# A third plain unit per later feed-forward stage, paired first blocks in the down projections, and modulation products moved

## The chip, the cores and the metric

The kernel runs on one core of one Trainium2 chip. The metric is the device time of one execution in microseconds (us). Tables and rows name the engines as the profile does: PE is TensorE (matmuls), PEld its weight loads, DVE is VectorE, ACT is ScalarE, SP is SyncE, which here only starts DMAs.

## The reference

The computation is a two-layer encoder on one sequence of 512 tokens, 1024 channels wide. Each layer has a feed-forward stage, a mixer and a second feed-forward stage, all on a residual stream `x` and all modulated by a conditioning vector `c`:

```python
def adaln_in(x, g, m, i):
    return rmsnorm(x, g) * (1 + m[:, i, 1][:, None]) + m[:, i, 0][:, None]

def swiglu(h, w1, w3, w2):
    return (jax.nn.silu(h @ w1) * (h @ w3)) @ w2

def reference(x, c, ...):
    cond = jax.nn.silu(c)
    for l in range(DEPTH):
        m = (cond @ w_mod[l] + b_mod[l]).reshape(bsz, 3, 3, D_MODEL)
        x = x + 0.5 * m[:, 0, 2][:, None] * swiglu(adaln_in(x, norm_g[l, 0], m, 0), ...)
        h = adaln_in(x, norm_g[l, 1], m, 1) @ w_in[l]
        ...   # mixer: attention beside a short convolution (layer 0) or a long FFT convolution (layer 1)
        x = x + m[:, 1, 2][:, None] * (mix @ w_out[l])
        x = x + 0.5 * m[:, 2, 2][:, None] * swiglu(adaln_in(x, norm_g[l, 2], m, 2), ...)
    return x
```

The hidden width of a feed-forward stage is 2752: 21 blocks of 128 columns (numbers 0 to 20) and a half block of 64 (number 21). All inputs are float32. The modulation `m` is the product of one vector with `w_mod` (75 MB), which the kernel takes in 144 pieces of 512 KB.

## The kernel before

**Arithmetic.** Every float32 operand is split into a high part in a 4-byte reduced format (`fp32r`) and the rest, and a product takes three matmuls: high by high, high by low, low by high (`mm3`, L222). A weight tile arrives by DMA in a `raw` buffer (four of them); ACT casts it to `wh` (L203) and DVE subtracts to get `wl` (L204). There are five buffers each of `wh` and `wl`.

**Stages.** There are six in a row: feed-forward (0,0), the mixer of layer 0, feed-forward (0,2), feed-forward (1,0), the mixer of layer 1, feed-forward (1,2). The last three feed-forward stages are "later" ones below. Each has three groups g0, g1, g2 of hidden blocks (`GROUPS`, L32: 6, 8 and 8 blocks), and each group has an up phase (L619 to L651) and a down projection (`project`, L347).

**Up phase.** A block is computed in one of two ways. A *plain* unit is two sums of 24 matmuls of 512 columns (L636 to L641). A *seven-product* unit (`up_seven`, L480) uses a Strassen-like scheme with seven products of 12 matmuls of 256 columns, 84 in all; its extra sums of weights are made by DVE (L456, L457, L462, L465), and sums over halves of the tokens once per stage by `token_sums` (L397) and `first_sum` (L435: it overwrites half of `h` with the sum T1, so no plain unit can follow it). `late_t1` puts the product that reads T1 last in its unit. A unit ends with the gated product (`glu`, L542, or `finish`, L510), which gives a pair of tiles in buffers `ga`, `gb`, `gc`; the last unit of a group makes it in two halves of tokens (L518 to L527). In g0 of a later stage, blocks 0 and 1 are plain, then comes the half block 21, then `token_sums` and `first_sum`, then blocks 2, 3 and 4 by seven products.

**Down projection.** For each of eight output blocks `dt`, all hidden blocks of the group (six or eight inputs, three matmuls of 512 columns each; the half block two) are summed in one of two PSUM banks of tag C (L365 to L368), one block in one bank and the next in the other, and DVE adds the result to `x` (`update`, L362), which frees the bank. The last projection of a stage (g2) does blocks 4 to 7 in halves of 256 columns and starts the next norm.

**Modulation products.** `gemv` (L232) starts a 512 KB DMA of `w_mod` into a `raw` buffer and has DVE multiply and sum it (L248). `rate` (L570) says how many are asked for per output block of the projections of g0, g1, g2; `in_up` (L571) in which groups one more is asked for ahead of each up unit.

**Order.** A scheduling framework places the instructions on each engine from priorities and buffer counts; on the chip each engine runs its list in order and waits on semaphores. The order of the code is not the order of the lists, so both are shown where it matters.

## Time and profile before

| | |
|---|---|
| median of 3 runs | 1894.36 us (1890.97 to 1896.87) |
| profiled execution | 1898.68 us, of which 1896.9 us span and 1.8 us around it |
| PE busy | 1831.8 us, 97% of the span, 11736 matmuls |
| DVE busy | 1547.3 us, 82% |
| ACT busy | 987.9 us, 52% |
| DMA | 269.23 MB, mean 142 GB/s |

The shares are means over the whole span. Phases are told by windows of the trace: a window gives its length, the busy time and number of instructions of each engine, the granted clock of TensorE as a share of 2.4 GHz (0.50 is 1.2 GHz), and what the DMA engines did. Matmuls overlap in the records, so a matmul's duration is longer than its step to the next one.

### The profile page before, as it was taken

What the parts mean: (1) busy time and instruction counts of PE and PEld (TensorE: products, weight loads), DVE (VectorE), ACT (ScalarE), POOL (GpSimd) and SP (SyncE); (2) the same over time, 40 slices, a digit from 0 to 9 for tenths busy, and PEclk for the clock granted to TensorE, in tenths of its full rate; (3) what the DMA queues carried; (4) which work ended last, traced back from release to release, by engine and by line L of the source; (5) the groups of instructions that cost most, each with busy time, mean ns of one, the idle gap of its engine ahead of it and who ended that gap; (6) DMA issues with size and microseconds to landing.
All of it is one profiled execution on the core that took longest, in us unless ns stands there. A gap on an engine that the chain in (4) does not pass through costs nothing.

```text
span 1896.9 us, 29947 instructions
## 1 busy us (share of the span) xinstructions
PE 1831.8 (97%) x11736; PEld 1642.3 (87%) x11736; DVE 1547.3 (82%) x2634; ACT 987.9 (52%) x1625; POOL 3.6 (0%) x9
## 2 busy tenths in 40 slices
PE   7999999899998999999989999999999998999999
PEld 5789899787788899898888988979887898898997
DVE  7987889787859978888898997987887879696682
ACT  4435345275947445254553554565788365354461
POOL 0000000000000000000000000000000000000000
PEclk9999999999999999999999999999999998999999
DMA  7752745833321634725516364445222322333231
GB/s 260 270 175 90 263 159 167 308 104 99 96 95 45 200 101 135 254 90 200 190 50 226 135 213 138 144 154 182 79 79 94 124 88 72 105 103 123 81 129 58
DMA packets 83655, 269.23 MB, mean 142 GB/s; under 512 B 10024, under 2 KB 13352, under 8 KB 83514
## 3 DMA queue, kind: packets, MB, share of 16 engines
q1 hardware_dynamic: 81898, 263.13, 41.4%
q0 software_dynamic: 1616, 4.20, 0.6%
q8 instruction: 92, 1.51, 0.3%
q14 instruction: 49, 0.40, 0.1%
HBM read 258.88 MB, written 10.50 MB: 142 GB/s over the span
## 4 chain that ended last, share of the span: by engine, by line
PE 79%; DVE 12%; DMA 5%; ACT 2%; issue 1%; SPq 0%; ACTq 0%; DVEq 0%
PE pA L476 26%; PE pC L358 20%; PE pV L476 4%; PE pA L358 4%; DVE wl L204 3%; DMA raw<-w2b 3%; PE pC L225 2%; PE pC L224 2%; PE pC L226 2%; DVE raw L248 2%; PE pA L225 2%; PE pA L226 2%; PE pA L224 2%; DMA raw<-w_mod 1%; ACT wh L203 1%
## 5 line engine op out<-in xcount | busy, mean ns | idle before, releaser
L203 ACT CAST wh<-raw 128x1024 fp32r<-128x1024 f32 (+2 forms) x390 | 371.6, 954 | 484.4 <-PE pA L476 137.1
L204 DVE TENSOR_TENSOR wl<-raw,wh 128x1024 fp32r<-128x1024 f32 (+2 forms) x390 | 429.7, 1104 | 97.1 <-ACT wh L203 92.2
L476 PE MATMUL pA<-e,wh 128*128 128x256 f32 x1680 | 309.2, 282 | 2.6 <-ACT tl L501 2.5
L476 PE MATMUL pA<-h,wh 128*128 128x256 f32 x1680 | 309.1, 282 | 0.4 <-DVE tc L528 0.4
L476 PEld LDWEIGHTS pA<-e,wh 128*128 128x128 f32 x1680 | 257.6, 189 | 7.3 <-ACT tl L501 3.8
L476 PEld LDWEIGHTS pA<-h,wh 128*128 128x128 f32 x1680 | 259.9, 191 | 1.7 <-DVE tc L528 0.6
L476 PE MATMUL pA<-h,wl 128*128 128x256 f32 x840 | 238.2, 284 | 19.2 <-DVE wl L204 19.2
L358 PE MATMUL pC<-gb,wh 128*128 128x512 f32 (+1 forms) x800 | 231.7, 374 | 7.6 <-ACT gb L203 4.5
L476 PE MATMUL pA<-e,wl 128*128 128x256 f32 x840 | 234.9, 280 | 0.0
L358 PE MATMUL pC<-ga,wh 128*128 128x512 f32 (+1 forms) x648 | 186.3, 376 | 9.3 <-DVE x L362 7.4
L248 DVE SCALAR_TENSOR_TENSOR raw<-raw,cond 128x1024 f32<-128x1024 f32 x144 | 174.9, 1220 | 17.3 <-DMA raw<-w_mod 16.6
L358 PEld LDWEIGHTS pC<-gb,wh 128*128 128x128 f32 x800 | 147.1, 193 | 38.1 <-ACT gb L203 5.9
L476 PEld LDWEIGHTS pA<-h,wl 128*128 128x128 f32 x840 | 159.3, 190 | 19.8 <-DVE wl L204 19.8
L476 PEld LDWEIGHTS pA<-e,wl 128*128 128x128 f32 x840 | 158.4, 189 | 0.0
L358 PEld LDWEIGHTS pC<-ga,wh 128*128 128x128 f32 x648 | 118.2, 193 | 34.6 <-issue 11.6
L358 PE MATMUL pC<-gb,wl 128*128 128x512 f32 (+1 forms) x392 | 145.7, 372 | 0.0
L362 DVE SCALAR_TENSOR_TENSOR x<-pC,mod,x 128x512 f32<-128x512 f32 (+1 forms) x108 | 74.1, 686 | 74.5 <-PE pC L358 74.3
L358 PE MATMUL pC<-ga,wl 128*128 128x512 f32 (+1 forms) x300 | 111.7, 372 | 0.0
L476 PE MATMUL pV<-h,wh 128*128 128x256 f32 x560 | 104.3, 285 | 1.3 <-DVE tc L547 1.3
L203 ACT CAST wh<-e 128x1024 fp32r<-128x1024 f32 x70 | 73.1, 1044 | 60.1 <-DVE e L462 33.5
L225 PE MATMUL pA<-h,wh 128*128 128x256 f32 (+1 forms) x333 | 102.9, 316 | 1.2 <-DVE h L345 1.2
L226 PE MATMUL pA<-h,wl 128*128 128x256 f32 (+1 forms) x333 | 102.7, 313 | 0.0
(317 smaller groups left out, 3620.5 us busy)
## 6 DMA issues: line engine op xcount, KB each, us to landing
raw<-w SPq DMA_DIRECT2D x164, 512.0 KB, 3.5
raw<-w_mod SPq DMA_DIRECT2D x144, 512.0 KB, 4.5
raw<-w2b SPq DMA_DIRECT2D x64, 512.0 KB, 4.1
raw<-w_in SPq DMA_DIRECT2D x36, 512.0 KB, 4.3
raw<-w2a SPq DMA_DIRECT2D x32, 384.0 KB, 3.6
raw<-w_out SPq DMA_DIRECT2D x16, 512.0 KB, 3.5
raw<-w_start SPq DMA_DIRECT2D x8, 512.0 KB, 4.8
xs<-x SPq DMA_DIRECT2D x16, 256.0 KB, 2.5
```

Of the source, the lines that this page charges most:

```text
L203: self.nc.scalar.copy(out=hi, in_=src)
L204: self.nc.vector.tensor_sub(out=lo, in0=src, in1=hi.bitcast(F32))
L224: mm(out, lhsT=wh, rhs=rh, start=start, stop=False)
L225: mm(out, lhsT=wh, rhs=rl, start=False, stop=False)
L226: mm(out, lhsT=wl, rhs=rh, start=False, stop=stop)
L248: nc.vector.scalar_tensor_tensor(out=raw, in0=raw, scalar=1.0, in1=self.cond, op0=ALU.mult, op1=ALU.mult, accum_out=m[:, c : c + 1])
L358: nc.tensor.matmul(ps, lhsT=lh, rhs=r, start=q == 0, stop=q == len(todo) - 1)
L362: nc.vector.scalar_tensor_tensor(out=x, in0=ps, scalar=gate[dt], in1=x, op0=ALU.mult, op1=ALU.add)
L476: self.nc.tensor.matmul(out, lhsT=lh, rhs=rr, start=first and n == 0, stop=n == 11, skip_group_check=True)
```

## The change

Three edits are made.

1. In the three later feed-forward stages block 2 becomes a plain unit; `first_sum` follows it, and block 3 is the first seven-product unit, with `late_t1`.
2. All twelve feed-forward down projections are called with `joint=True`: output blocks 0 and 1 take both C banks, every input but the last is multiplied for block 0, then for block 1, and then the last input for each. In g0 the half block is put ahead of block 4, so that block 4 is the last input.
3. The modulation products: (0,0) and (0,2) ask for one instead of two per output block in g2. One per up unit is asked for in g1 and g2 of (0,0) (before: g2 alone), in g1 and g2 of (0,2) (before: none) and in g1 of (1,0) (before: g1 and g2). There are 144 in all, as before.

```diff
-    def project(self, n_in, weight, rhs, gate, key, order=None, bank="C", gemv=0):
+    def project(self, n_in, weight, rhs, gate, key, order=None, bank="C", gemv=0, joint=False):
...
-        def products(ps, w, c0, c1):
-            todo = []
-            for k in order:
-                todo += rhs[k](self.block(w, k), c0, c1)
-            for q, (lh, r) in enumerate(todo):
-                nc.tensor.matmul(ps, lhsT=lh, rhs=r, start=q == 0, stop=q == len(todo) - 1)
+        def products(ps, w, c0, c1, a=0, b=n_in):
+            for k in range(a, b):
+                todo = rhs[order[k]](self.block(w, order[k]), c0, c1)
+                for q, (lh, r) in enumerate(todo):
+                    nc.tensor.matmul(
+                        ps, lhsT=lh, rhs=r, start=k == 0 and q == 0, stop=k == n_in - 1 and q == len(todo) - 1)
...
         nfull = 4 if key else KT
+        pair = []
+        if joint:
+            for dt in range(2):
+                pair.append((weight(dt), self.ps("C")))
+                products(pair[dt][1], pair[dt][0], 0, T, 0, n_in - 1)
         for dt in range(nfull):
-            w = weight(dt)
-            ps = self.ps(bank[dt % len(bank)])
-            products(ps, w, 0, T)
+            if dt < len(pair):
+                w, ps = pair[dt]
+                products(ps, w, 0, T, n_in - 1)
+            else:
+                w = weight(dt)
+                ps = self.ps(bank[dt % len(bank)])
+                products(ps, w, 0, T)
             update(dt, ps, 0, T)
             self.gemv(gemv)
...
-        rate = {(0, 0): (1, 2, 2), (0, 2): (1, 2, 2), (1, 0): (1, 1, 0), (1, 2): (0, 0, 0)}[l, i]
-        in_up = {(0, 0): (2,), (1, 0): (1, 2)}.get((l, i), ())
+        rate = {(0, 0): (1, 2, 1), (0, 2): (1, 2, 1), (1, 0): (1, 1, 0), (1, 2): (0, 0, 0)}[l, i]
+        in_up = {(0, 0): (1, 2), (0, 2): (1, 2), (1, 0): (1,)}.get((l, i), ())
...
                     if not first:
                         self.token_sums()
-                        self.first_sum()
-                elif first and (g == 0 or f < 8):
+                elif f < 8 and first or f == 2:
...
-                    if f == 7:
+                    if f == (7 if first else 2):
                         self.first_sum()
...
-                        late_t1=f == (8 if first else 2), halves=f == fs[-1])
+                        late_t1=f == (8 if first else 3), halves=f == fs[-1])
...
-            self.project(len(rhs), weight, rhs, self.gate[l, i], key if g == 2 else None, gemv=rate[g])
+            self.project(
+                len(rhs), weight, rhs, self.gate[l, i], key if g == 2 else None, gemv=rate[g],
+                order=[0, 1, 2, 3, 5, 4] if g == 0 else None, joint=True)
```

The next pieces are read from the lists of the two kernels; lines are those of each kernel (a line of `token_sums` or of `up_seven` is ten higher in the changed one, the update is L363 there).

**PE, the start of the down projection of (0,2) g1.** `gc` is the last input, `pC_1391` the bank of output block 0; that of block 1 is `pC_1397` before and `pC_1395` in the change. First before, the end of block 0 and the start of block 1:

```order
L358 MATMUL pC_1391_7793<-gb_1351_7499,wh_1389_7788 128x512
L358 MATMUL pC_1391_7793<-gb_1350_7498,wl_1390_7789 128x512
L358 MATMUL pC_1391_7793<-gc_1369_7626,wh_1389_7788 128x512
L358 MATMUL pC_1391_7793<-gc_1370_7627,wh_1389_7788 128x512
L358 MATMUL pC_1391_7793<-gc_1369_7626,wl_1390_7789 128x512
L358 MATMUL pC_1397_7831<-ga_1236_6760,wh_1395_7826 128x512
L358 MATMUL pC_1397_7831<-ga_1237_6761,wh_1395_7826 128x512
L358 MATMUL pC_1397_7831<-ga_1236_6760,wl_1396_7827 128x512
```

And of the change, from the end of block 1's other inputs to the start of block 2:

```order
L358 MATMUL pC_1395_7788<-gb_1348_7457,wh_1393_7783 128x512
L358 MATMUL pC_1395_7788<-gb_1349_7458,wh_1393_7783 128x512
L358 MATMUL pC_1395_7788<-gb_1348_7457,wl_1394_7784 128x512
L358 MATMUL pC_1391_7760<-gc_1368_7588,wh_1389_7755 128x512
L358 MATMUL pC_1391_7760<-gc_1369_7589,wh_1389_7755 128x512
L358 MATMUL pC_1391_7760<-gc_1368_7588,wl_1390_7756 128x512
L358 MATMUL pC_1395_7788<-gc_1368_7588,wh_1393_7783 128x512
L358 MATMUL pC_1395_7788<-gc_1369_7589,wh_1393_7783 128x512
L358 MATMUL pC_1395_7788<-gc_1368_7588,wl_1394_7784 128x512
L358 MATMUL pC_1403_7837<-ga_1228_6701,wh_1401_7832 128x512
L358 MATMUL pC_1403_7837<-ga_1229_6702,wh_1401_7832 128x512
```

The last input stands behind 42 matmuls instead of 21, and the two banks close three matmuls apart, directly ahead of block 2, which needs the first of them again.

**DVE, the same place.** From the last block's gated product to the update of `x` by output block 0 (L362 before). First before:

```order
L204 TENSOR_TENSOR wl_1402_7865<-raw_1400_7863,wh_1401_7864 128x1024
L204 TENSOR_TENSOR gc_1370_7627<-tc_1380_7643,gc_1369_7626 128x256
L523 TENSOR_TENSOR tc_1380_7643<-pA_1387_7701,tl_1378_7641 128x256
L248 SCALAR_TENSOR_TENSOR raw_1404_7895,mod_1_0_0_6555<-raw_1404_7895,cond_75 128x1024
L525 SCALAR_TENSOR_TENSOR tc_1380_7643<-tq_1379_7642,tc_1380_7643 128x256
L248 SCALAR_TENSOR_TENSOR raw_1405_7898,mod_1_0_0_6555<-raw_1405_7898,cond_75 128x1024
L204 TENSOR_TENSOR gc_1370_7627<-tc_1380_7643,gc_1369_7626 128x256
L204 TENSOR_TENSOR wl_1408_7903<-raw_1406_7901,wh_1407_7902 128x1024
L362 SCALAR_TENSOR_TENSOR x_973_5254<-pC_1391_7793,mod_0_2_16_3445,x_973_5254 128x512
```

And of the change (the update is L363):

```order
L535 SCALAR_TENSOR_TENSOR tc_1380_7610<-tq_1379_7609,tc_1380_7610 128x256
L248 SCALAR_TENSOR_TENSOR raw_1404_7863,mod_1_0_16_7816<-raw_1404_7863,cond_75 128x1024
L204 TENSOR_TENSOR gc_1369_7589<-tc_1380_7610,gc_1368_7588 128x256
L248 SCALAR_TENSOR_TENSOR raw_1405_7866,mod_1_0_16_7816<-raw_1405_7866,cond_75 128x1024
L204 TENSOR_TENSOR wl_1408_7871<-raw_1406_7869,wh_1407_7870 128x1024
L248 SCALAR_TENSOR_TENSOR raw_1410_7901,mod_1_0_16_7816<-raw_1410_7901,cond_75 128x1024
L248 SCALAR_TENSOR_TENSOR raw_1411_7904,mod_1_0_16_7816<-raw_1411_7904,cond_75 128x1024
L261 TENSOR_TENSOR mod_1_0_16_7816<-mod_1_0_16_7816,cols_76 128x8
L264 TENSOR_SCALAR mod_1_0_16_7816<-mod_1_0_16_7816 128x8
L363 SCALAR_TENSOR_TENSOR x_973_5254<-pC_1391_7760,mod_0_2_16_3359,x_973_5254 128x512
L363 SCALAR_TENSOR_TENSOR x_974_5255<-pC_1395_7788,mod_0_2_16_3359,x_974_5255 128x512
L204 TENSOR_TENSOR wl_1414_7911<-raw_1412_7909,wh_1413_7910 128x1024
```

Between the last block's last product (L525, L535) and the first update there stand one L248 before and four now, and the two updates now follow each other. One more L248 stands just ahead of the rows shown of the change.

**DVE, (0,2) g0, around the first seven-product unit before and block 2 as a plain unit now.** `e1`, `e2`, `tq` and `h` are the token sums, `wl_1145` is the first weight tile of block 2 in both kernels. First before:

```order
L204 TENSOR_TENSOR h_1034_5677<-e3_1110_6062,h_1033_5676 128x256
L417 SCALAR_TENSOR_TENSOR tq_1135_6119<-tq_1136_6120,th_1134_6117 128x256
L549 TENSOR_TENSOR ga_1104_6023<-tc_1109_6055,ga_1103_6022 64x512
L204 TENSOR_TENSOR e1_1138_6126<-tq_1136_6120,e1_1137_6125 128x512
L552 CAST ga_1104_6023<-ga_1104_6023 64x512
L204 TENSOR_TENSOR e2_1132_6112<-tq_1135_6119,e2_1131_6111 128x256
L204 TENSOR_TENSOR h_1036_5679<-e3_1110_6062,h_1035_5678 128x256
L204 TENSOR_TENSOR h_1038_5681<-e3_1110_6062,h_1037_5680 128x256
L204 TENSOR_TENSOR h_1040_5683<-e3_1110_6062,h_1039_5682 128x256
L456 TENSOR_TENSOR e3_1143_6143<-raw_1142_6142 128x512
L204 TENSOR_TENSOR wl_1145_6149<-raw_1141_6141,wh_1144_6148 128x1024
```

And of the change:

```order
L557 TENSOR_TENSOR tc_1109_6055<-tc_1109_6055,pA_1108_6030 64x512
L424 SCALAR_TENSOR_TENSOR tq_1136_6120<-e3_1110_6062,th_1134_6117 128x256
L204 TENSOR_TENSOR wl_1145_6137<-raw_1143_6135,wh_1144_6136 128x1024
L559 TENSOR_TENSOR ga_1104_6023<-tc_1109_6055,ga_1103_6022 64x512
L427 SCALAR_TENSOR_TENSOR tq_1135_6119<-tq_1136_6120,th_1134_6117 128x256
L562 CAST ga_1104_6023<-ga_1104_6023 64x512
L204 TENSOR_TENSOR e1_1138_6126<-tq_1136_6120,e1_1137_6125 128x512
L204 TENSOR_TENSOR e2_1132_6112<-tq_1135_6119,e2_1131_6111 128x256
L204 TENSOR_TENSOR wl_1148_6167<-raw_1146_6165,wh_1147_6166 128x1024
```

The first weight tile of block 2 moves ahead of nine instructions of token sums and half-block work, and the weight sum L456 ahead of it is gone; the four splits of T1 into `h` go behind block 2 altogether.

## Rows read from the trace of the kernel before

**Rows 1.** The page: busy time of each engine.

```profile
PE 1831.8 (97%) x11736; PEld 1642.3 (87%) x11736; DVE 1547.3 (82%) x2634; ACT 987.9 (52%) x1625; POOL 3.6 (0%) x9
```

**Rows 2.** Windows, up phase of g0: start:end, length, busy (count), clock, DMA share, GB/s.

```profile
605.58:645.54 39.96, 33.02 (x256) 32.58 (x255) 38.41 (x66) 21.67 (x35) 0.00 (x0) 0.87 0.36 120
966.25:1005.29 39.04, 32.11 (x257) 31.64 (x255) 38.05 (x66) 21.51 (x35) 0.00 (x0) 0.91 0.36 121
1574.54:1614.69 40.15, 33.49 (x256) 32.84 (x255) 36.00 (x61) 21.93 (x36) 0.00 (x0) 0.87 0.31 96
```

**Rows 3.** Windows: eight seven-product units of (1,2) g1; three plain units of (0,0) g1.

```profile
1645.78:1725.77 79.99, 79.99 (x676) 79.74 (x675) 67.09 (x103) 46.74 (x72) 0.00 (x0) 1.00 0.35 113
121.92:155.21 33.29, 33.29 (x145) 27.05 (x144) 21.74 (x32) 10.98 (x17) 0.00 (x0) 1.00 0.31 98
```

**Rows 4.** Timeline, (0,2) g0: start, us, engine, line, operation, tiles [idle before <-releaser].

```profile
605.81 0.39 PE L476 MATMUL pV<-h,wh 128*128 128x256 f32 x2
607.17 0.41 DVE L414 SCALAR_TENSOR_TENSOR tq<-e,th 128x256 f32<-128x256 f32 x1
...
611.85 1.22 DVE L204 TENSOR_TENSOR wl<-raw,wh 128x1024 fp32r<-128x1024 f32 x1
...
613.13 0.58 PE L476 MATMUL pA<-h,wl 128*128 128x256 f32 x1 [6.93 <-DVE wl L204]
```

**Rows 5.** Windows: granted clock after two idle stretches of PE.

```profile
608.20:618.40 10.20, 5.27 (x24) 5.27 (x25) 10.14 (x18) 4.97 (x8) 0.00 (x0) 0.50 0.00 0
1010.90:1014.30 3.40, 3.18 (x8) 2.51 (x9) 2.39 (x5) 0.17 (x1) 0.00 (x0) 0.50 0.54 181
```

**Rows 6.** Windows: down projections of g0, stages (0,0), (0,2), (1,0), (1,2).

```profile
84.33:121.92 37.59, 34.57 (x137) 27.29 (x136) 34.28 (x62) 12.60 (x17) 0.00 (x0) 0.91 0.71 232
645.54:680.17 34.63, 32.57 (x135) 26.09 (x134) 26.47 (x43) 8.24 (x11) 0.00 (x0) 0.95 0.58 192
1005.29:1040.18 34.89, 32.46 (x136) 26.00 (x135) 29.47 (x49) 8.24 (x11) 0.00 (x0) 0.95 0.66 219
1614.69:1645.78 31.09, 31.02 (x136) 24.85 (x135) 20.48 (x32) 7.95 (x10) 0.00 (x0) 1.00 0.34 110
```

**Rows 7.** Windows: down projections of g1, stages (0,0) and (0,2).

```profile
205.54:253.21 47.67, 45.71 (x192) 36.54 (x190) 40.14 (x61) 11.00 (x13) 0.00 (x0) 0.96 0.78 265
760.87:804.81 43.94, 43.91 (x192) 35.42 (x190) 36.02 (x56) 9.75 (x11) 0.00 (x0) 1.00 0.76 260
```

**Rows 8.** Windows: projections of g2, (0,0) and (0,2); a mixer's of like shape.

```profile
334.90:380.18 45.28, 38.80 (x209) 33.62 (x208) 31.91 (x54) 12.61 (x19) 1.24 (x1) 0.92 0.87 311
885.37:927.35 41.98, 37.07 (x207) 32.16 (x205) 31.69 (x52) 12.88 (x19) 0.00 (x0) 0.96 0.75 263
531.07:566.67 35.60, 35.59 (x208) 31.09 (x207) 17.20 (x25) 11.40 (x17) 0.00 (x0) 1.00 0.22 74
```

**Rows 9.** Timeline of PE, start of the projection of (1,0) g0.

```profile
1008.06 0.63 PE L358 MATMUL pC<-ga,wh 128*128 128x512 f32 x2
1011.12 0.80 PE L358 MATMUL pC<-gb,wh 128*128 128x512 f32 x1 [2.43 <-ACT gb L203]
```

**Rows 10.** Waits of the whole run: us in total, times, longest.

```profile
PE pC L358 <- DVE x L362: 7.4, 3, 4.2
DVE raw L248 <- DMA raw<-w_mod: 16.6, 23, 3.1
```

**Rows 11.** Timeline, projection of (0,0) g2: one modulation product on DVE.

```profile
363.81 1.22 DVE L248 SCALAR_TENSOR_TENSOR raw<-raw,cond 128x1024 f32<-128x1024 f32 x1
```

**Rows 12.** Timeline, projection of (1,2) g2: first block's last matmul and its update.

```profile
1853.94 0.40 PE L358 MATMUL pC<-gc,wl 128*128 128x512 f32 x1
...
1854.38 0.75 DVE L362 SCALAR_TENSOR_TENSOR x<-pC,mod,x 128x512 f32<-128x512 f32 x1 [1.02 <-PE pC L358]
```

**Rows 13.** Windows: up phases of (0,0) g2 and (0,2) g1.

```profile
253.21:334.90 81.69, 80.82 (x675) 79.42 (x674) 75.92 (x121) 45.85 (x71) 0.00 (x0) 1.00 0.47 157
680.17:760.87 80.70, 80.16 (x677) 79.71 (x675) 70.47 (x110) 45.73 (x71) 0.00 (x0) 1.00 0.37 120
```

More of the change, by code (lines that the diff above doesn't have):

```diff
@@ L638, in ffn @@
                             self.mm3(ps[s], self.block(w, kt), self.h[kt], kt == 0, kt == KT - 1)
-                        if g == 0:
+                        if first and g == 0:
                             self.gemv(4)
```

## The prediction

> **What bounds the kernel now.** I read the page's busy times first. PE is busy 1831.8 of 1896.9 us and every other engine less than 83% [rows 1], so what there is to win is idle time of PE, 65 us by that row, and time at a lower clock; some of both lies at the start and in the mixers, which the change leaves alone. Then I cut the feed-forward stages into phases with windows and compared phases that do the same work. A seven-product unit takes 80.0 / 8 = 10.0 us and a plain unit 33.3 / 3 = 11.1 us where nothing disturbs them [rows 3]. Against that:
>
> - The up phase of g0 in a later stage is three seven-product units, 30.0 us, and takes 39.96, 39.04 and 40.15 us [rows 2]: 10.0, 9.0 and 10.2 us lost, 29.2 together. The timeline shows where: PE starts the first unit at 605.81, has only high weights, and waits 6.9 us for the first `wl`, which DVE starts at 611.85 because the token sums stand ahead of it [rows 4]. Then the granted clock is 0.50, that is 1.2 GHz, for 10.2 us, part of it idle [rows 5].
> - The down projection of g0 takes 31.1 us in (1,2), where no modulation products run, and 37.6, 34.6 and 34.9 us in the other three [rows 6]: 6.5, 3.5 and 3.8 us lost. In g1, (0,0) takes 47.7 us against 43.9 in (0,2) [rows 7]: 3.7 us. The mechanism by the timeline: from 1008.06 to 1011.12 PE waits for `gb`, the last gated product, as 21 or fewer matmuls of the first output block are too short to cover it [rows 9], and again 3.4 us follow at 0.50 [rows 5].
> - In g2, (0,0) and (0,2) take 45.3 and 42.0 us against 35.6 for a mixer's projection of like shape and nearly the same count of matmuls [rows 8]: 9.7 and 6.4 us. Here two products per output block stand in DVE's list and PE waits for the update that frees a bank, 7.4 us in three waits, the longest 4.2 [rows 10].
>
> Together the projections lose 33.6 us in six places.
>
> **Part 1, block 2 plain.** Its price is 11.1 - 10.0 = 1.1 us of PE in each of three stages. In the changed list of DVE the first `wl` of block 2 stands right behind the sum that starts at 607.17 [rows 4], so it can start near 607.5 and end near 608.7. PE has two long and two short matmuls before it needs it and falls idle near 606.3: a wait of 2.4 us instead of 6.9. The second weight comes after some 3.4 us more of DVE work, inside the 5.5 us that PE needs for the first half. The four T1 splits move behind block 2 and are needed last in block 3. I count slow clock behind it, as behind the wait of 2.43 us in g0's projection [rows 9]: 3.4 us at half [rows 5], worth 1.7. So a stage loses 1.1 + 2.4 + 1.7 = 5.2 instead of 9.7, and three stages gain 29.2 - 15.6 = 13.6 us. Bounds: no wait and no slow clock give 29.2 - 3.3 = 25.9; the wait as long as before (a `wl` that again sits behind the sums) gives 29.2 - 3 x (1.1 + 9.7) = -3.2. I take 13.6, since the place of the `wl` is read from the list.
>
> **Part 2, two blocks together.** The last gated product is now wanted after 42 matmuls of 0.23 us (43.9 us for 192 [rows 7]), 9.7 us, in g0 after 28, 6.4 us. The longest lateness so far was about 3 us past five or seven inputs, so these waits end. What is late next is output block 2: it needs bank 0 again, which closes only 6 matmuls (1.4 us) before. Its update stands in DVE's list behind more than before: in (0,2) g1 five L248 and two `wl` from the last block's first gated step on, where two L248 and two `wl` stood. At 1.22 us for an L248 [rows 11] or a `wl` [rows 4] and some 0.4 us for a small step I sum DVE's work ahead of the first update to (0,0): 7.3, 10.3, 8.9 us for g0, g1, g2; (0,2): 7.8, 10.4, 8.9; (1,0): 7.8, 12.9, 16.6; (1,2): 3.9 in each. The pair, with its last inputs, covers 11.1 us (g0: 7.8), from the end of the up phase; about 1.1 us go for the start of DVE's list and the update itself. So the bank is late by 0.4 us in g2 of (0,0) and (0,2), 0.4 to 1.1 us in g0 and g1 of (0,2) and g0 of (1,0), 2.9 us in g1 of (1,0), and by what DMAs add: L248 waited 16.6 us in 23 cases for its `raw` [rows 10], mostly in such projections, and in (0,0) the DMA share is the highest (0.71 to 0.87 [rows 6 to 8]). I put 3.5 us on g0 and g1 of (0,0), 1.3 on g0 and 1.5 on g1 of (0,2), 1.3 on g0 of (1,0), 2.8 on g1 of (1,0), 3 on its g2, where the filter's own matmuls fill part of 6.6. Slow clock adds 1.7 at the four largest and 0.6 at each of the other three: 8.6. In (1,2), where nothing is queued, the first block's last matmul starts at 1853.94 and the update at 1854.38 ends 0.75 later [rows 12]: 1.2 us, of which three matmuls and the last one's own 0.23 cover 0.9. That leaves 0.35 to 0.4 there and in g2 of (0,0) and (0,2): five times, 2.0 us. Sum: 16.9 + 8.6 + 2.0 = 27.5 us of new waits. Bounds: 12 x 0.4 = 4.8 us if DVE is never late; eight times the longest wait for an update, 4.2 [rows 10], with 1.7 of slow clock, 47 us, plus 2 is 49.
>
> The Trainium skill (Perfetto Trace Analysis, Optimizing Tensor Performance, Matmuls) says that independent groups of matmuls should rotate through PSUM banks, so that one is emptied while the next group runs; the pair breaks this, as both banks close together. The trace agrees as far as it goes [rows 12]: the emptying that was hidden there is 0.4 us in the open, 4.8 us for twelve projections by that rule alone.
>
> **Part 3, modulation products.** With one product per block in g2 of (0,0) and (0,2), DVE has 1.3 us less per output block, and the bank waits there go, as in the g1 projection at rate 1 of (1,0). I leave 0.5 us in each. So the 33.6 us of projections become 27.5 + 1.0 = 28.5: a gain of 5.1 us for parts 2 and 3. The products that move to up phases are hidden behind 10 us units unless DVE fills up: an up phase with one per unit took 81.7 us against 80.7 without [rows 13]. Three phases get them and one loses them: 2 x 1.0 = 2.0 us lost. Bounds: 0 and, if PE must wait for the whole 1.3 us in 16 more units, 21; the nearest row says 1.0 per phase. DVE is busy 75.9 of 81.7 us there, so the cover is nearly spent.
>
> **The sum.** 13.6 + 5.1 - 2.0 = 16.7 us off the profiled execution's 1898.7 us: 1882. This execution is 4.3 us above the median of the runs, so the median comes to 1894.4 - 16.7 = 1877.7; the bank waits that I took from bounds far apart are sized rather high, so I round down to 1876 us.
>
> **Rivals.**
> (a) *The pair costs only the turn of the banks.* DVE's small steps overlap with waits for ACT anyway, so the lists may be shorter in time than my sums, and the waits for block 2 stay at 0.4 us: 33.6 - 4.8 - 1.0 = 27.8 instead of 5.1, total 39: 1855. As (0,0), with the highest DMA share, will keep some of its two waits, I take 1859. For it: where nothing is queued the loss is 0.4. Against: an update has waited behind L248 already [rows 10, 11].
> (b) *The plain unit does not shorten the wait in g0.* ACT must cast the weight before DVE can subtract, and ACT has the casts of the token sums too. Part 1 is then -3.2 and the sum about 0: 1894.
> (c) *Slower: block 2 waits for its bank behind the products.* Place: the first update of the eight projections that have products or filter work. Price: at 4.2 + 1.7 us each plus 2.0, 49 us against 33.6 lost now; with the other parts 33.6 - 49 - 1 + 13.6 - 2.0 = -5: 1899. It decides from about 5.3 us for each of the eight, slow clock included.
>
> The same page's section Identifying Performance Opportunities reads repeated gaps on the busiest engine as a sign of too little PSUM for the next tile, which is what (c) would look like; no run so far shows it in this form.
>
> **How the numbers follow.** Chances: forecast 0.48, (a) 0.25, (b) 0.14, (c) 0.13. Forecast and (a) are faster nearly always. (b) and (c) split: of (b) half is faster, as one or two stages would still gain, and half within the bound; of (c) four in ten within, and half slower. A measurement of this kernel tells changes over 0.3% (5.7 us) from none. Faster 0.81, same 0.12, slower 0.07. The forecast's own range is 1866 to 1886; taking in most of (a) and (b) it is 1856 to 1892.
>
> **What would show it.** Part 1 is right if the wait of the first `wl` in g0 of the later stages is 2 to 3 us and the phase near 35 us; wrong if it is still over 5. Part 2 is right if no wait for `ga`, `gb` or `gc` is left in the projections and PE's waits for `x` rise from 7.4 us in three to some 15 to 20 us, all at the third output block; (a) if they are under 7, (c) if over 33. Part 3 is right if the g2 projections of (0,0) and (0,2) come to about 36 us and the up phases with products to 81 or 82. Waits of DVE for `raw` in up phases, or of PE for `wl` in g1 and g2 of (0,2), would make the forecast wrong on the slow side.

## The result, and the profile after

The changed kernel takes 1873.72 us (median of 4 runs, 1871.36 to 1875.81), the kernel before 1895.61 in the same session: a ratio of 0.9887 with a 95% interval of [0.9863, 0.9912]. Two later sessions gave 0.9908 [0.9887, 0.9929] and 0.9891 [0.9873, 0.9910]. The forecast was 1876 us, 18.4 us below the median known then; measured are 17.8 to 21.9 us below the kernel before. The total is right. The account below shows that the first of its three parts is right in its mechanism and near in size, and that the other two come out at the forecast size by errors that cancel.

The profiled execution took 1871.36 us, with a span of 1869.6 us. It is the fastest of these four runs, while that of before (1898.68) is slower than every other run of that kernel; so this pair is 27.3 us apart, more than the medians, and a second profile of before follows among the experiments. First the granted clock over the run, of before and then of after (core, span, mean share of 2.4 GHz):

```profile
core 0: 1896.9 us, clock 0.986
```

```profile
core 0: 1869.6 us, clock 0.995
```

At two levels, 1.0 and 0.5, a mean of 0.986 is 1896.9 x 0.014 x 2 = 53 us at the lower one, and 0.995 is 19 us.

**Part 1, g0 of the later stages.** Windows of after, from the first matmul of block 2 to the end of the up phase (start:end, length, busy and count per engine, clock, DMA share, GB/s):

```profile
597.55:634.08 36.53, 33.88 (x221) 30.62 (x219) 32.84 (x55) 17.79 (x32) 0.00 (x0) 0.95 0.38 123
951.65:986.12 34.47, 32.55 (x220) 29.51 (x219) 32.58 (x55) 17.90 (x32) 0.00 (x0) 1.00 0.42 131
1552.67:1586.51 33.84, 32.40 (x221) 29.52 (x219) 30.40 (x51) 18.44 (x32) 0.00 (x0) 1.00 0.36 113
```

They answer to [rows 2]: 36.5, 34.5 and 33.8 us for 40.0, 39.0 and 40.2, a gain of 14.3 us. The timeline of the first of them, for [rows 4]:

```profile
599.21 0.41 DVE L424 SCALAR_TENSOR_TENSOR tq<-e,th 128x256 f32<-128x256 f32 x1
...
599.55 1.21 DVE L204 TENSOR_TENSOR wl<-raw,wh 128x1024 fp32r<-128x1024 f32 x1
...
600.82 0.50 PE L226 MATMUL pA<-h,wl 128*128 128x512 f32 x1 [1.94 <-DVE wl L204]
```

The low weight follows the sum L424 at once, and PE waits 1.94 us for it where it waited 6.93. Over the three stages these waits are 3.9 us, so some 1.0 in each of the other two; the granted clock falls behind the long one (0.95) and stays at 1.00 in the others.

**The down projections.** Windows of after: g0 of (0,0), (0,2), (1,0), then g1 of (0,0) and (0,2), then g2 of (0,0) and (0,2).

```profile
83.09:118.73 35.64, 33.04 (x137) 26.53 (x136) 33.42 (x61) 12.41 (x17) 0.00 (x0) 0.95 0.74 253
634.08:665.41 31.33, 30.96 (x136) 24.90 (x134) 29.29 (x49) 8.39 (x11) 0.00 (x0) 1.00 0.74 245
986.12:1017.58 31.46, 30.98 (x135) 24.91 (x134) 29.32 (x49) 8.27 (x11) 0.00 (x0) 1.00 0.72 246
202.82:247.82 45.00, 44.87 (x193) 35.51 (x192) 37.59 (x57) 10.71 (x13) 1.24 (x1) 1.00 0.82 282
747.35:793.72 46.37, 43.94 (x192) 35.39 (x191) 38.28 (x59) 10.58 (x12) 0.00 (x0) 1.00 0.79 274
340.58:375.98 35.40, 35.09 (x207) 30.49 (x205) 23.11 (x39) 12.55 (x18) 0.00 (x0) 1.00 0.66 224
877.46:912.72 35.26, 35.08 (x206) 30.48 (x205) 22.95 (x38) 12.12 (x18) 0.00 (x0) 1.00 0.56 194
```

Against [rows 6 to 8] six of seven are shorter, by 2.0, 3.3, 3.4, 2.7, 9.9 and 6.7 us; g1 of (0,2) is 2.4 us longer. In sum 25.5 us less. No wait for `ga`, `gb` or `gc` is left in this profile; in the two later ones of the changed kernel one for `gb` comes back in g0 of (0,0), of 1.47 and 0.26 us. The third output block does wait for its bank, as the list had it; here it is in g1 of (0,2), the last matmul of the pair and the first of block 2:

```profile
757.50 0.40 PE L358 MATMUL pC<-gc,wl 128*128 128x512 f32 x1
760.33 0.73 PE L358 MATMUL pC<-ga,wh 128*128 128x512 f32 x2 [2.43 <-DVE x L363]
```

**The up phases behind them.** Windows of after: g2 of (0,0), g1 and g2 of (0,2).

```profile
247.82:340.58 92.76, 83.64 (x677) 82.45 (x675) 77.94 (x124) 45.87 (x72) 0.00 (x0) 0.94 0.50 164
665.41:747.35 81.94, 81.59 (x677) 80.28 (x675) 75.20 (x122) 45.11 (x70) 0.00 (x0) 1.00 0.47 152
793.72:877.46 83.74, 81.69 (x677) 80.21 (x676) 76.55 (x123) 46.38 (x72) 0.00 (x0) 1.00 0.48 159
```

Here 15.5 of the 25.5 us went back, by this pair of profiles: the first of them took 81.69 us before, the second 80.70 [rows 13], the third 80.56 (from the end of g1's window in [rows 7] to the start of g2's in [rows 8]). That is 11.1, 1.2 and 3.2 us. A second profile of the kernel before (under the experiments) has 85.5 us for the first, and with it 7.2 for the 11.1. PE's waits show one new long one, in the first of these phases:

```profile
PE pA L486 <- DVE tq L518: 7.4, 2, 6.8
PE pC L358 <- DVE x L363: 6.6, 8, 2.6
PE pA L486 <- ACT tq L517: 4.8, 5, 1.4
```

The chain of waits in that place runs back to a DMA of weights that took 6.89 us (start, us, what):

```profile
253.64 6.89 DMA raw<-w
260.53 0.02 issue
260.55 0.04 DVE e L466
...
265.10 1.01 PE pA L486 x3
```

And the DMA issues from 240 to 262 us show what is beside it (KB each, median us from issue to landing):

```profile
vec<-vec POOLq DMA_DIRECT2D x1, 2048.0 KB, 19.2
raw<-w SPq DMA_DIRECT2D x3, 512.0 KB, 9.6
```

`vec<-vec` spreads the first mixer's bias table (`rel_bias`, called behind g2's up phase in the code of both kernels). The scheduler now starts it at 241.13 us, where g1's projection ends; before it started at 337.58, inside g2's projection.

**The first mixer,** whose code is untouched. Windows of before and of after:

```profile
392.88:531.07 138.19, 134.74 (x709) 110.67 (x708) 110.27 (x236) 103.92 (x226) 0.00 (x0) 1.00 0.31 101
```

```profile
388.67:523.05 134.38, 133.59 (x710) 110.37 (x708) 110.82 (x237) 107.04 (x229) 0.00 (x0) 1.00 0.33 104
```

It is 3.8 us shorter. Nothing of this stood in the forecast.

### The profile page after: what moved, and what is told of

Its sections match the earlier page's. It is cut to its first block, busy times and chain, and to the rows that moved or that the text cites. A ratio compares the mean times of both kernels' runs of the same rounds, so it can differ in the third digit from the quotient of the medians.

```text
span 1869.6 us, 29686 instructions
## 1 busy us (share of the span) xinstructions
PE 1827.3 (98%) x11628; PEld 1630.7 (87%) x11628; DVE 1527.1 (82%) x2604; ACT 980.6 (52%) x1610; POOL 3.6 (0%) x9
## 4 chain that ended last, share of the span: by engine, by line
PE 72%; DVE 15%; DMA 9%; ACT 2%; issue 2%; SPq 0%; ACTq 0%; DVEq 0%
PE pA L486 23%; PE pC L358 16%; DVE wl L204 4%; PE pA L358 4%; PE pV L486 4%; DMA raw<-w_mod 3%; DVE raw L248 3%; PE pC L225 2%; PE pC L226 2%; PE pC L224 2%; PE pA L226 2%; DMA raw<-w2b 2%; PE pA L225 2%; PE pA L224 2%; DMA raw<-w 2%
## 5 line engine op out<-in xcount | busy, mean ns | idle before, releaser
L203 ACT CAST wh<-raw 128x1024 fp32r<-128x1024 f32 (+2 forms) x387 | 368.8, 956 | 453.5 <-PE pA L486 134.4
L486 PE MATMUL pA<-h,wh 128*128 128x256 f32 x1608 | 297.2, 283 | 8.5 <-DVE tq L518 7.4
L486 PE MATMUL pA<-e,wh 128*128 128x256 f32 x1608 | 295.5, 281 | 5.7 <-ACT tq L517 4.8
L486 PEld LDWEIGHTS pA<-h,wh 128*128 128x128 f32 x1608 | 247.5, 190 | 12.3 <-DVE tq L518 7.8
L486 PEld LDWEIGHTS pA<-e,wh 128*128 128x128 f32 x1608 | 245.8, 189 | 10.8 <-ACT tq L517 8.6
L486 PE MATMUL pA<-h,wl 128*128 128x256 f32 x804 | 226.6, 282 | 0.2 <-DVE wl L204 0.2
L486 PE MATMUL pA<-e,wl 128*128 128x256 f32 x804 | 224.4, 279 | 0.0
L248 DVE SCALAR_TENSOR_TENSOR raw<-raw,cond 128x1024 f32<-128x1024 f32 x144 | 175.1, 1220 | 31.1 <-DMA raw<-w_mod 29.7
L486 PEld LDWEIGHTS pA<-h,wl 128*128 128x128 f32 x804 | 151.5, 188 | 0.5 <-DVE wl L204 0.4
L486 PEld LDWEIGHTS pA<-e,wl 128*128 128x128 f32 x804 | 151.3, 188 | 0.0
L358 PEld LDWEIGHTS pC<-ga,wh 128*128 128x128 f32 x648 | 115.2, 189 | 33.6 <-DVE x L363 12.3
L363 DVE SCALAR_TENSOR_TENSOR x<-pC,mod,x 128x512 f32<-128x512 f32 (+1 forms) x108 | 73.2, 685 | 83.1 <-PE pC L358 82.6
L226 PE MATMUL pA<-h,wl 128*128 128x256 f32 (+1 forms) x373 | 118.7, 324 | 3.9 <-DVE wl L204 3.9
L225 PE MATMUL pA<-h,wh 128*128 128x256 f32 (+1 forms) x373 | 119.3, 327 | 1.3 <-DVE h L345 1.3
L224 PE MATMUL pA<-h,wh 128*128 128x256 f32 (+1 forms) x373 | 116.0, 323 | 0.0
```

The costliest lines, as they stand in the source:

```text
L203: self.nc.scalar.copy(out=hi, in_=src)
L224: mm(out, lhsT=wh, rhs=rh, start=start, stop=False)
L225: mm(out, lhsT=wh, rhs=rl, start=False, stop=False)
L226: mm(out, lhsT=wl, rhs=rh, start=False, stop=stop)
L248: nc.vector.scalar_tensor_tensor(out=raw, in0=raw, scalar=1.0, in1=self.cond, op0=ALU.mult, op1=ALU.mult, accum_out=m[:, c : c + 1])
L358: nc.tensor.matmul(ps, lhsT=lh, rhs=r, start=k == 0 and q == 0, stop=k == n_in - 1 and q == len(todo) - 1)
```

## The experiments

Each profile was cut at the same matmuls: "(0,0)" from its first down projection to the first mixer, "mixer" from there to its output projection, "g0 up" as the sum over the three later stages from the same place of the stage to its first down projection, "(0,2)" and "(1,0)" from the first down projection to that place of the next stage. A mixer or a stage is taken to begin at the first matmul behind the second pair of L303, the sums of its norm. All in us. The ratio, with its interval, is that to the kernel before in the same session, over all runs; it can differ from that of the two medians by 0.1%. The last five rows are of experiments that follow.

| kernel | ratio, 95% interval | (0,0) | mixer | g0 up | (0,2) | (1,0) | bias DMA |
|---|---|---|---|---|---|---|---|
| before | 1 | 308.6 | 138.2 | 197.8 | 294.5 | 313.9 | g2 projection |
| before, again | one run | 305.1 | 139.7 | 197.3 | 290.1 | 314.0 | g2 projection |
| edit 1 alone | 0.9929 [0.9912, 0.9947] | 307.7 | 139.5 | 182.7 | 290.4 | 313.0 | as before |
| edit 2 alone | 0.9989 [0.9978, 1.0] | 308.0 | 134.4 | 197.5 | 289.2 | 312.5 | end of g1 |
| edit 3 alone | 0.9999 [0.9986, 1.0012] | 300.8 | 144.1 | 198.1 | 292.8 | 311.5 | g2 projection |
| edits 1 and 2 | 0.9895 [0.9874, 0.9917] | 312.5 | 134.3 | 183.8 | 287.6 | 312.6 | end of g1 |
| all three | 0.9887 [0.9863, 0.9912] | 305.6 | 134.4 | 183.5 | 291.3 | 311.2 | end of g1 |
| all three, 2nd | 0.9908 [0.9887, 0.9929] | 309.2 | 134.4 | 183.5 | 293.2 | 313.5 | end of g1 |
| all three, 3rd | 0.9891 [0.9873, 0.9910] | 304.8 | 134.3 | 183.6 | 290.8 | 311.5 | end of g1 |
| bias early | 0.9887 [0.9868, 0.9906] | 301.9 | 134.4 | 184.0 | 293.7 | 311.9 | g1 up phase |
| bias early, again | 0.9869 [0.9854, 0.9883] | 303.6 | 134.3 | 182.1 | 292.3 | 312.4 | g1 up phase |
| four banks | 0.9910 [0.9891, 0.9929] | 299.8 | 139.5 | 184.1 | 290.7 | 320.7 | g2 projection |
| edit 1, products of (0,0) | 0.9901 [0.9885, 0.9917] | 301.4 | 143.9 | 181.0 | 293.7 | 312.8 | g2 projection |
| edits 1, 2, products of (0,0), bias early | 0.9855 [0.9832, 0.9878] | 302.6 | 134.4 | 182.0 | 288.0 | 312.5 | g1 up phase |

**Edit 1 alone.**

```diff
-                        self.first_sum()
-                elif first and (g == 0 or f < 8):
+                elif f < 8 and first or f == 2:
...
-                        late_t1=f == (8 if first else 2), halves=f == fs[-1])
+                        late_t1=f == (8 if first else 3), halves=f == fs[-1])
```

Expected: 

> The kernel before with edit 1 alone (block 2 of the later stages plain, T1 sums behind it). Theory: the first low weight comes ahead of the token sums, the wait of 6.9 us in g0 shrinks to about 2 us in each of three stages, net of 1.1 us more PE work 14 us in all: about 1880 us against 1894. Rival (the weight is still late, because ACT and DVE have the same work to do): no gain, 1894 to 1897.

Measured: 1878.18 us against 1893.77, 15.6 us less by the medians and 13.4 by the ratio. The three g0 phases give 15 us in the profile; the other phases are within 1 us of what the two profiles of the kernel before show. The theory holds, the rival falls. By the ratios this edit is two thirds to three quarters of the whole gain.

**Edit 2 alone.** The kernel before with `joint=True` and the order of inputs in g0.

```diff
+        if joint:
+            for dt in range(2):
+                pair.append((weight(dt), self.ps("C")))
+                products(pair[dt][1], pair[dt][0], 0, T, 0, n_in - 1)
```

Expected: 

> The kernel before with edit 2 alone (two output blocks together, half block ahead of block 4; two products per block kept in g2). Theory: the waits for the last gated product go (about 9 to 11 us in the g0 projections and g1 of (0,0)), and the third block's wait for its bank costs back 3 to 6; the 2 MB DMA that spreads the bias moves from the g2 projection of (0,0) to the start of its up phase and costs up to 11 us there while the projection gets back some 5: in sum 1886 to 1896. Rival (the recorded forecast): 27 us of new bank waits, slower than before by 5 us or more, 1900.

Measured: 1890.81 us against 1893.77, 3 us less, and its interval touches 1. The bank waits are 12.5 us, with the wait near 262 us behind the bias DMA:

```profile
PE pC L358 <- DVE x L363: 12.5, 10, 3.5
PE pQ L315 <- DVE acc L293: 5.9, 1, 5.9
PE pA L486 <- DVE tq L518: 5.3, 1, 5.3
```

So the recorded size of 27 us is refuted, also where two products per block are left in g2; so is the 3 to 6 us that I expected here. The feed-forward stages together do not gain clearly: (0,0), (0,2) and (1,0) are 909.7 us, against 917.0, 909.1 and 911.1 in the three profiles that have this code as before. The mixer gains 4 to 5.

**Edit 3 alone.**

```diff
-        rate = {(0, 0): (1, 2, 2), (0, 2): (1, 2, 2), (1, 0): (1, 1, 0), (1, 2): (0, 0, 0)}[l, i]
-        in_up = {(0, 0): (2,), (1, 0): (1, 2)}.get((l, i), ())
+        rate = {(0, 0): (1, 2, 1), (0, 2): (1, 2, 1), (1, 0): (1, 1, 0), (1, 2): (0, 0, 0)}[l, i]
+        in_up = {(0, 0): (1, 2), (0, 2): (1, 2), (1, 0): (1,)}.get((l, i), ())
```

Expected: 

> The kernel before with edit 3 alone (modulation products). Theory: the projections of g2 in (0,0) and (0,2) lose their bank waits (9 to 13 us of the 16 lost there), the up phases that get products lose 2 to 6 us: 1885 to 1888. Rival (the loss in g2 of (0,0) is the 2 MB DMA of the bias, which stays in that projection here): (0,0) g2 stays over 40 us long and the gain is under 5 us, 1890.

Measured: 1892.72 us against 1893.77, no difference: I expected 6 to 9 us. Windows: the g2 projections of (0,0) and (0,2), the up phases of (0,2) g1 and g2, the mixer.

```profile
333.11:371.26 38.15, 36.41 (x209) 30.90 (x208) 22.98 (x39) 12.21 (x19) 1.24 (x1) 1.00 0.74 264
886.36:922.48 36.12, 35.08 (x206) 30.51 (x205) 22.81 (x36) 12.72 (x19) 0.00 (x0) 1.00 0.56 189
674.54:758.35 83.81, 81.70 (x676) 80.33 (x675) 77.34 (x126) 46.18 (x71) 0.00 (x0) 1.00 0.50 160
802.01:886.36 84.35, 81.76 (x676) 80.31 (x675) 77.94 (x125) 45.89 (x71) 0.00 (x0) 1.00 0.49 161
383.95:528.04 144.09, 138.78 (x709) 113.48 (x708) 111.62 (x237) 104.66 (x227) 0.00 (x0) 0.96 0.31 97
```

The projections gain as expected, 7 and 6 us against [rows 8], although the bias DMA still runs in the first of them, so the rate is what held them up. But each up phase that gets products is 3 us longer than the 81.3 and 81.0 us of edit 1 alone, where they have none, and the mixer takes 144.1 us. (0,0), (0,2) and (1,0) together come to 905.1 us, 4 to 12 below the three profiles named under edit 2, and the mixer takes 4.4 to 5.9 of that back.

**The changed kernel with the bias table asked for early.**

```diff
-            if (l, i, g) == (0, 0, 2):
-                self.rel_bias()
...
+                if (l, i, f) == (0, 0, 10):
+                    self.rel_bias()
```

Expected: 

> The changed kernel with the bias table (three small loads, one matmul, one add, a 2 MB spreading DMA) asked for in g1 of (0,0) at block 10 instead of after g2's up phase. Theory: the wait of 6.8 us at 258 us and the slow clock behind it are this DMA beside the weight loads; the up phase of (0,0) g2 falls from 92.8 to 82 us and the total to about 1863. Rival: the wait comes from the modulation products queued on DVE; the up phase stays over 90 us and the total at 1874.

Measured: 1870.98 us, 0.9887 [0.9868, 0.9906], far from 1863. The wait and the slow clock are gone and the up phase of g2 is 84.3 us, as expected but for 2 us, but the profiled total equals that of the changed kernel. As another session can hide a few us, I ran both side by side. Expected of the changed kernel there: 

> The changed kernel a third time, as the yardstick for the three kernels beside it on the same chip: 0.989 to 0.991 of the kernel before (two sessions gave 0.9887 and 0.9908). The wait of 5 to 7 us near 260 us, behind the bias DMA, comes back; PE waits for x 6 to 12 us.

Expected of the other: 

> The changed kernel with the bias table asked for at block 10 of (0,0) g1, once more, beside the changed kernel itself. Theory: the wait of 5 to 7 us near 260 us is gone and the up phase of (0,0) g2 is 84 us instead of 90 to 93, but the DMA costs 2 to 4 us in the g1 projection instead: 3 to 5 us below the changed kernel. Rival: what the up phase gains the other phases lose, within 1.5 us of it.

Measured: 1874.17 and 1869.52 us, ratios 0.9891 [0.9873, 0.9910] and 0.9869 [0.9854, 0.9883]: 4.7 us by the medians, as expected, though the intervals overlap; the two executions that were profiled differ by 0.7 us (1869.87 and 1869.17). So a gain in the total is likely and not shown. The up phase of g2, of the changed kernel and of this one:

```profile
249.56:339.66 90.10, 82.72 (x676) 81.70 (x675) 77.70 (x124) 45.85 (x72) 0.00 (x0) 0.96 0.51 166
```

```profile
255.05:337.97 82.92, 80.97 (x677) 80.07 (x675) 75.45 (x121) 45.93 (x71) 0.00 (x0) 1.00 0.49 154
```

7 us come back here. The phase starts 5.5 us later, though: 2.3 of these are in g0's projection, ahead of the DMA, which now starts at 178.46, and are no price of it; for the rest, behind it, the runs don't tell. Over all profiles the phase says more: it takes 89.1 to 92.8 us in the five where this DMA starts at the end of g1's projection, and 81.7 to 85.7 in the nine where it starts elsewhere, some 6 to 7 us less on the mean.

**A second profile of the kernel before.** The same program, no edit.

Expected: 

> The kernel before, once more, for a second profile of the same program. Theory: its losses in the projections with modulation products are not fixed by the lists but by when DMAs land; where the first profile lost 3.5 to 4.0 us (g1 of (0,0), g0 of (0,2) and of (1,0)) this one will differ by 2 us or more in at least one of the three, while the 9 to 10 us of g0's up phases come back within 0.5 us. Rival: every phase comes back within 0.5 us, and the differences between profiles are the edits'.

Measured (one run, 1890.78 us): windows of the projections of (0,2) g0, (0,0) g1, (0,0) g2 and (0,2) g2, and of the up phases of (0,2) g0 and of (0,0) g2.

```profile
642.77:675.44 32.67, 30.99 (x136) 24.92 (x134) 26.34 (x43) 8.24 (x11) 0.00 (x0) 1.00 0.62 204
202.04:245.97 43.93, 43.93 (x192) 35.28 (x191) 35.98 (x56) 9.65 (x11) 0.00 (x0) 1.00 0.79 263
331.49:375.67 44.18, 39.56 (x209) 34.17 (x208) 31.92 (x54) 12.49 (x19) 1.24 (x1) 0.92 0.93 317
881.07:920.16 39.09, 35.57 (x206) 30.61 (x205) 31.03 (x52) 12.58 (x18) 0.00 (x0) 1.00 0.82 281
602.58:642.77 40.19, 33.26 (x256) 32.81 (x255) 38.51 (x66) 21.63 (x35) 0.00 (x0) 0.87 0.37 118
245.97:331.49 85.52, 82.06 (x676) 79.91 (x674) 78.85 (x126) 46.05 (x71) 0.00 (x0) 1.00 0.50 162
```

The theory holds in the main: g0's up phase comes back to 0.2 us in (0,2) and to 0.5 in (1,0), while the projections are 2.0, 3.7, 1.1 and 2.9 us shorter than in the first profile. In (1,2) it is 1.1 us shorter (39.0), with the same waits for the first `wl` in both profiles (6.9, 6.9 and 5.3 us) and a granted clock of 0.91 for 0.87; there the 0.5 us was missed. What PE loses in the projections is not a property of the lists alone, and the up phase of (0,0) g2, 81.69 us in the first profile, takes 85.52 here without any edit (85.19 with edit 1 alone).

**The changed kernel, second session.** Expected: 

> The changed kernel, once more, for a second profile and for times on the same chip as the next two. Theory: the wait near 258 us and the up phase of 92.8 us in (0,0) g2 depend on when the bias DMA lands and come back at least half; total 1870 to 1874.

Measured: 1878.01 us against 1895.84. The wait comes back with 5.5 us, the up phase with 90.6; the total is 4 us above the range that I expected.

**Block 2 on another bank.**

```diff
+                order=[0, 1, 2, 3, 5, 4] if g == 0 else None, joint=True, bank="CCQQ")
```

Expected: 

> The changed kernel with the output blocks behind the pair rotating over four PSUM banks, two of tag Q (idle in these stages) and two of tag C, so that block 2 need not wait for block 0's update. Theory: PE's waits for x (6.6 us in the changed kernel's profile) go to under 1.5 us: 1866 to 1869. Rival: the update is late anyway and the wait moves to block 4 or to the next weights: within 2 us of the changed kernel.

Measured: 1877.98 us, the same as the changed kernel beside it. PE's waits for `x`, 11.2 us there, are gone from the list of its longest waits, so these waits were the bank. But the total gains nothing: the up phases of (0,2) behind them are longer than the 81.9 and 83.7 us of after and the 82.5 and 83.8 of the kernel beside it,

```profile
663.83:746.98 83.15, 81.07 (x676) 80.02 (x675) 76.47 (x125) 45.01 (x70) 0.00 (x0) 1.00 0.50 156
790.65:876.27 85.62, 81.04 (x676) 80.05 (x675) 79.11 (x127) 46.00 (x71) 0.00 (x0) 1.00 0.51 158
```

the projection of (1,0) g2 gets a new wait of 5.45 us for a weight, and the scheduler put the bias DMA back behind g2, with a mixer of 139.5 us. Against the changed kernel beside it, (0,0) is 9.4 us shorter and (0,2) 2.5, (1,0) is 7.2 longer and the mixer 5.0. In (1,0) the banks of tag Q are not idle, as I had taken them to be: the filter's matmuls write `pQ` there (L1007, L1029); whether that brings the new wait was not tried. So in these stages the test shows the wait's cause and not what its removal alone is worth.

In (1,2), where nothing is queued, the test is clean. The projection of g1, after and then on four banks:

```profile
1697.61:1741.69 44.08, 43.92 (x191) 35.43 (x190) 20.89 (x28) 8.73 (x11) 0.00 (x0) 1.00 0.26 87
```

```profile
1705.97:1749.63 43.66, 43.66 (x191) 35.48 (x190) 20.92 (x28) 8.71 (x11) 0.00 (x0) 1.00 0.28 88
```

The kernel before took 43.67. The turn of the banks costs 0.4 us here, and as much in g0 (31.12 and 30.71) and in g2 (47.99 and 47.55).

**Edits 1 and 2, products as before.**

```diff
-        rate = {(0, 0): (1, 2, 1), (0, 2): (1, 2, 1), (1, 0): (1, 1, 0), (1, 2): (0, 0, 0)}[l, i]
-        in_up = {(0, 0): (1, 2), (0, 2): (1, 2), (1, 0): (1,)}.get((l, i), ())
+        rate = {(0, 0): (1, 2, 2), (0, 2): (1, 2, 2), (1, 0): (1, 1, 0), (1, 2): (0, 0, 0)}[l, i]
+        in_up = {(0, 0): (2,), (1, 0): (1, 2)}.get((l, i), ())
```

Expected: 

> The kernel before with edits 1 and 2; the products stay as before (two per block in g2 of (0,0) and (0,2)). Theory: up phases of (0,2) are 2.5 us shorter each than in the changed kernel, the two g2 projections 2 to 4 us longer, so edit 3 is worth nearly nothing here: 1874 to 1877. Rival (edit 3 takes the bank waits that edit 2 would otherwise meet): 1880 or more.

Measured: 1875.52 us, 2.5 us below the changed kernel beside it, with overlapping intervals: on top of edits 1 and 2, edit 3 gains nothing. It gains 3 us or more in (0,0) (312.5 against 305 to 309) and loses 3 to 6 in (0,2) (287.6 against 291 to 293).

That says where to cut. Edit 3 moves products only within (0,0), where `rate` and `in_up` ask for 48 before and after, and from (1,0) to (0,2), 8 of them. So the (0,0) part can be had alone.

**Edit 1 and the (0,0) part of edit 3, without pairs.**

```diff
-        rate = {(0, 0): (1, 2, 2), (0, 2): (1, 2, 2), (1, 0): (1, 1, 0), (1, 2): (0, 0, 0)}[l, i]
-        in_up = {(0, 0): (2,), (1, 0): (1, 2)}.get((l, i), ())
+        rate = {(0, 0): (1, 2, 1), (0, 2): (1, 2, 2), (1, 0): (1, 1, 0), (1, 2): (0, 0, 0)}[l, i]
+        in_up = {(0, 0): (1, 2), (1, 0): (1, 2)}.get((l, i), ())
```

Expected: 

> The kernel before with edit 1, and of edit 3 only what concerns (0,0): one product per output block in g2, one per up unit in g1 and g2; the other stages ask for products as before, and there are no paired blocks. The bias DMA stays in the g2 projection. Theory: (0,0) gains 5 to 7 us over edit 1 alone, (0,2) keeps its old time: 5 us below edit 1 alone, which makes it 0.990 of the kernel before or less, and no slower than the changed kernel. Rival (edit 2 is needed for what edits 1 and 3 gain): 0.993.

Measured: 1876.80 us, 0.9901 [0.9885, 0.9917]. (0,0) falls to 301.4 us, 6 less than with edit 1 alone, as expected, but the mixer takes 143.9 us, as with edit 3 alone, 4.3 more. So it is 2.6 us above the changed kernel and not clearly better than edit 1 alone.

**Edits 1 and 2, the (0,0) part of edit 3, and the early bias table.** The last diff, in the changed kernel, with that of the bias table.

Expected: 

> Edits 1 and 2, of edit 3 only what concerns (0,0), and the bias table asked for at block 10 of (0,0) g1. Theory: (0,2), from the start of its g0 projection to its end, falls from 291 to 294 us to 287 to 289, (0,0) from 305 to 309 us (same start) to 302 to 304, (1,0) is unchanged: 6 to 9 us below the changed kernel, about 0.985 of the kernel before. Rival (time is only moved between phases, as DVE and the loads bound these stages as a whole): within 2 us of the changed kernel.

Measured: 1865.12 us (1864.21 to 1872.05), 0.9855 [0.9832, 0.9878], against 1874.17 for the changed kernel beside it: 9 us less, the lowest median of all kernels run, though the intervals touch. (0,0) takes 302.6, the mixer 134.4, (0,2) 288.0 and (1,0) 312.5 us. From the changed kernel with the early bias table (0.9869, beside it) it differs only in the products of (0,2) and (1,0): 4.4 us less by the medians with overlapping intervals, (0,2) 4.3 us shorter and (1,0) the same. So the rival, that time only moves between phases, does not hold for the (0,2) part of edit 3. The up phases of (0,2) g1 and g2, now without products, run at PE's pace:

```profile
661.85:741.75 79.90, 79.90 (x676) 79.65 (x675) 69.50 (x108) 44.70 (x70) 0.00 (x0) 1.00 0.37 117
787.20:867.10 79.90, 79.90 (x677) 79.65 (x675) 69.28 (x108) 44.77 (x70) 0.00 (x0) 1.00 0.37 114
```

## Why the prediction was right, point by point

**Part 1 (forecast 13.6 us, measured 14.3 in the profile; alone 13.4 by the ratio and 15.6 by the medians): the mechanism is right, and the size has some luck in it.** The place of the `wl` was read from the list, its start 0.34 us behind the sum's came out as written, and the wait is 1.94 us in one stage and some 1.0 in two, for a forecast of 2.4 (its own test asked for 2 to 3). The slow clock was counted three times and came once. These two terms came to 5.7 us for 12.3 (3.9 of waits, and 36.5 us at 0.95, worth 1.8). The phases are yet 11.5 us longer than the 31.1 of two seven-product units and a plain one each, so 5.8 us have other sources that the forecast did not have; 2.1 of them are three matmuls of the projection that stand in each of these windows, 0.9 two waits for `tc` (L557), 1.2 two for `tq` (L517).

**Part 2, new waits for the bank (forecast 27.5 us): the mechanism is right, the term mis-sized.** The waits are there, at the third output block, for the reason given, and on four banks they go away. Where nothing is queued the turn of the banks costs 0.4 us, as forecast (0.35 to 0.4). The Trainium skill (Perfetto Trace Analysis, Optimizing Tensor Performance, Matmuls) says that independent groups of matmuls should rotate through different PSUM banks, so that one is emptied while the next runs. The runs agree with it: four banks take back those 0.4 us in (1,2), and the waits of 11.2 us in the other stages, though the total stayed at 1878.0. But these waits are 6.6, 11.2 and 8.8 us in three profiles, for 18.9 without the slow clock (its own test asked for 15 to 20). The step that failed is the sum of DVE's work ahead of the first update, taken as if all of it lay behind the end of the up phase. g0 of (0,0), priced at 3.5, waits 2.6 to 3.5 us, but g1 of (0,0), priced at 3.5 too, has no listed wait in the first profile, 1.8 us in the second and 0.8 in the third, and g1 and g2 of (1,0), priced at 2.8 and 3, have none. In (1,0) g1 the sum was 12.9 us; there the last block's first gated step ran 1.2 us ahead of the end of the up phase, the update started 11.1 us behind it, and four of the filter's matmuls (L1007, 2.1 us) kept PE busy meanwhile. Of the 8.6 us of slow clock some 2 came, in g0 of (0,0) (0.95 to 0.96 over the phase); in the second profile g1 of (0,0) shows 0.96 too.

**Parts 2 and 3, what the projections lost before (33.6 us): a price from one execution.** It stood on one profile. In the second one of the same program the projections of (0,2) g0, (0,0) g1, (0,0) g2 and (0,2) g2 alone lose 9.7 us less. The total of that run was 7.9 us lower, and not 9.7 or more, since other phases were longer, (0,0) g2's up phase by 3.8 us.

**Part 3, products in up phases (forecast 1.0 us a phase): mis-sized.** The g2 projections came to 35.4 and 35.3 us, as its test asked (about 36). The row taken for the up phases, [rows 13], was that of (0,0) g2 in one execution; the same two phases of the second profile are 85.5 and 81.1 us, 4.5 apart for 1.0. In (0,2) they cost 0.6 and 2.7 us in the changed kernel and 2.5 and 3.4 in edit 3 alone, both against the 81.3 and 81.0 of edit 1 alone, and 2.0 and 3.8 in the changed kernel against the 79.9 of the last experiment, where the blocks are paired too. (1,0) g2, which loses its products, gains 0.8 us (83.4 to 82.7).

**What the forecast did not have:** the scheduler moves the bias DMA when edit 2 changes the lists. This costs some 6 to 7 us in the up phase of (0,0) g2 (89.1 to 92.8 us in five profiles, 81.7 to 85.7 in the other nine), and with it goes a shorter mixer. In all eight profiles where that DMA starts before 250 us the mixer takes 134.3 to 134.4 us, in the six where it starts after 330 us 138.2 to 144.1; the kernel with four banks, which has the pairs but the DMA at 334.74, has 139.5. The timeline of SP shows what moves with it, the first load of the bias by the softmax, of before and of after:

```profile
449.97 0.90 SPq L787 DMA_DIRECT2D rb<-vec  x2
```

```profile
388.96 0.32 SPq L798 DMA_DIRECT2D rb<-vec  x1
```

In all eight the first such load starts 0.3 us behind the mixer's start, in all six 57 us behind it. The bias has landed long before in either case (at 360.5 us in before, where the mixer starts at 392.9), so it is not the transfer that the mixer waits for: what differs is where these loads stand. The fourteen profiles tie the place of the DMA to that of the loads and to the mixer's length. That the one causes the other is not shown, as no run moves the DMA alone in a kernel where it starts late; why the scheduler makes these lists was not tried.

**The sum.** (0,0), (0,2) and (1,0) together take 917.0, 909.1 and 911.1 us where parts 2 and 3 are absent, mean 912.4, and 908.2, 915.9 and 907.1 in the changed kernel, mean 910.4: 2.0 us for a forecast of 3.1, within what two profiles of one program differ by. The mixer adds 3.8 to 5.3, and the pairs cost 0.8 in (1,2). With part 1's 14.3 that is 19 to 21 us for a forecast of 16.7 to 18.4. Without the mixer, which the forecast did not have, it would be 15.5, about as near. In the pair of profiles first compared, the projections gained 25.5 for 5.1 and three up phases lost 15.5 for 2.0 in all: both terms wrong, and what is left of them is 10 for 3.1 in this pair and 2.0 over the six profiles. By its own test, bank waits under 7 us, rival (a) was met in the first profile (6.6), and yet its total of 1859 was not. The projections gained 25.5 us in that pair, near its 27.8, but it had no loss for the up phases beyond part 3's 2.0, and they lost 15.5: by the ranges above to the bias DMA, to the products that moved there, and to what two executions of one program differ by. Rivals (b) and (c) fell.

## What to carry to other kernels

When work of another engine is moved from one phase to the next, price it in the phase that receives it: the products asked for in (0,2)'s up phases cost PE 2.0 and 3.8 us there, where it runs without a wait when they are absent. That cost is not fixed by their number: with eight of them in g2's projection again and eight in (1,0), (0,2) is 4.3 us shorter, and (1,0) takes 312.5 us for 312.4. Take waits that hang on DMA landings from at least two profiles of the same program, and those that hang on an order in a list from one. Where a scheduler makes the lists, look through the whole difference of the lists for transfers that moved, in stages the edit does not touch too: here a 2 MB transfer that no edit names cost 6 to 7 us in one phase, and another stage was 4 to 10 us shorter in every profile where it started early.

## What the runs showed that was not expected

A weight load of 512 KB beside the 2 MB spreading DMA took 9.6 us to land (median of three), for 3.5 us in the same stretch of before; the profile counts 1040 packets of that DMA's queue there, at 25.3% of the engines' time, and 28.3% for the loads. The mean busy share of the DMA engines over the stretch is thus not much over a half, and yet the loads take nearly three times as long.
